# Two sums of the first two experts put off to later experts, the ranking of the experts inside the first gather, and the first four weight reloads singly

## The chip, the cores and the metric

The kernel runs on one core of a Trainium2 chip. Its time is device microseconds (us) of one execution; the times given are medians over runs. An expert's weights come from the chip's memory by DMA into the core's on-chip buffers; the matrix products run on TensorE (PE in the profile, PEld for its weight loads), element work on VectorE (DVE), ScalarE (ACT) and GpSimd (POOL); SyncE (SP) issues the weight DMAs, each when the buffer that it fills is free.

## The reference, cut to what matters

The program is a two-layer block (recurrent mixer, attention, two dense MLPs) followed by a third block (two attention-like branches, an output projection, a layer norm) and a mixture of experts (MoE). Sequence 256, width 1024, 32 experts, 4 experts for each token, all in float32. The change lies in the last part:

```
h = layer_norm(DEEPNORM_ALPHA * h + mix, ln1_g, ln1_b)
logits = h @ router_w + router_b
top_vals, top_idx = lax.top_k(logits, TOP_K)          # 4 of 32
gates = softmax(top_vals)
for each expert e, for the tokens routed to it:
    hcat = x @ w_up[e] + b_up[e]                      # 1024 -> 2048
    x_glu = minimum(hcat[:, 0::2], 7)
    x_lin = clip(hcat[:, 1::2], -7, 7)
    act = x_glu * sigmoid(1.702 * x_glu) * (x_lin + 1)
    y = act @ w_down[e] + b_down[e]                   # 1024 -> 1024
ffn = sum over a token's experts of gate * y
out = layer_norm(DEEPNORM_ALPHA * h + ffn, ln2_g, ln2_b)
```

All 32 experts' weights are read whole: 32 x 12 MB (8 MB up, 4 MB down).

## The kernel before, in words

Up to about 820 us of the span the dense layers run. Their weights are split into high and low parts (L406, L428) and multiplied in three products (L508 to L510); none of that is changed. What follows is the MoE, written for one expert after another in an order fixed at build time; a place in that order is called a position, 0 to 31.

**The work of a position.** U(p) is the first layer of position p: `first_layer` multiplies 64 token slots (`xT`) by eight chunks of the up weights, 1 MB each (L1777 into `hp`), after a product that lays the bias down (`first_bias`, L1577, which needs the one-hot column `sel`). D(p) is the second layer: four chunks of the down weights (L1838 into `py`). `PHASES` orders them U0, U1, D0, U2, D1, U3, D2 and so on. Behind U(p) TensorE turns the gates (`pG`, L1762) and gathers the tokens of position p+1 (`gather`, L1746 into `pX`), which DVE then scales into `xT` (L1749, L1750, in two halves). `gated` is the activation, `turned` its transpose (`paT`, L1820), `keep` scales D(p)'s result into `y` and `combine` adds it to the residual `x` (L1860 into `pC`, then DVE L1861).

**The stream of weights.** Chunks are numbered in the order of use (`ORDER`). The first 20 (20 MB) are loaded by `fill` while the dense layers still run, each as soon as some buffer is free. From then on chunk n goes into the buffer of chunk n-20 (`slots`), and `release(j)`, called behind each chunk's products, issues that load on SP (`load_to`, `load_chunk` L345). Buffers in `paired` take two chunks in one 2 MB DMA, so such a load is issued only when TensorE is through with both chunks of the pair. Chunk 20 is the first of position 2, whose expert number comes out of a table in memory (`ids`), read by SP at L365.

**Hooks.** `later[(p, j)]` lists functions called behind chunk j of position p (j from 8 on is the second layer). They hold the side work: `number_experts` (the table `ids`), `first_gather` (gather of position 0 in three pieces), `three_parts` (`x` split into three bf16 parts for the later gathers), `gates_of_tokens`, `by_token` and `by_position` (the token lists in the order of the positions, `prg` and `prp`), `residual_sum` (`x` times ln1's gain and a constant; the gain is spread over rows by products `pg`, L1924), `start_sum` (the down biases and ln1's bias added to `x` by products `pbd`, L1934, from `rows`, which POOL loads at L1995 and L1996), and `list_overflow`. `rank_experts` (products `pcnt`) orders the experts by token count; it stands between the first gather's second piece and U0.

**The end.** `sums` copies `x` into four PSUM banks by products with the identity (`fin`, L2110), `join` adds D30's result there, `last_norm` adds D31's and computes the last layer norm on DVE. A loop follows for experts with more tokens than slots.

Of the kernel before, what the change touches and what calls it, by code (L numbers as in the profile page):

```python
# [145 lines left out]
def fused(ctx: ExitStack, tc: tile.TileContext, d, out, dbg=None):  # L146
# [173 lines left out]
    stream = {"next": 0}  # L320
    chunk_of, expert_of, paired = {}, {}, []

# [33 lines left out]
    def load_to(n):  # L356

        while stream["next"] < min(n, 12 * NE):
            i = stream["next"]
            pl = slots[i % len(slots)]  # L360
            if pl in paired and n < i + 2:
                break
            pos, j = ORDER[i]
            if j == 0 and pos >= 2:
                e = sp.value_load(ids[0:1, pos:pos + 1], min_val=0, max_val=NE - 1)  # L365
                expert_of[pos] = ds(e, 1)
            stream["next"] += load_chunk(pl, pos, pos if pos < 2 else expert_of[pos], j)
# [850 lines left out]
    with ExitStack() as mixo, ExitStack() as attn:  # L1218
# [232 lines left out]
        paired.append(first)  # L1451
        fill((0, first), (2, first))
        state["ahead"] = 3
# [5 lines left out]
        assert state["loaded"] == TAKEN, (state["loaded"], len(plan))  # L1459
        fill((4, second), (6, parts_A[0]))  # L1460
        act.activation(gates[0], gates[0], AF.Sigmoid)
# [23 lines left out]
        paired.append(third)  # L1485
        fill((10, third))
        mb = ctx.enter_context(tc.tile_pool(name="bias", bufs=1, side="right", reuse_waits="tile"))
# [11 lines left out]
        paired.append(rawD)  # L1499
        fill((8, rawD))  # L1500
        n3 = mo.tile([128, 3, 2, D], BF, name="n3")
# [181 lines left out]

        keep_warm(4)
        pr = mm("prk").rearrange("p (a e) -> p a e", e=NE)
# [11 lines left out]
    slots = [first] * 4 + [second] * 2 + [parts_A[0]] * 2 + [rawD] * 2 + [third] * 2 + [parts_A[1]] * 2 + \  # L1697
        [rawC] * 2 + [parts_A[2], rawF] + [rawE] * 2
    stream["next"] = len(slots)

# [28 lines left out]
    def three_parts(t):  # L1729

        for c in range(2):
            s = slice(c * 512, (c + 1) * 512)
            r = wk.tile([128, 512], F32, name="r", tag=("xl", "sgm")[c], bufs=1)
            hi, mid, lo = [n3[:, i, t, s] for i in range(3)]
            act.copy(hi, x[:, t, s])
            dve.tensor_sub(r, x[:, t, s], hi)
            act.copy(mid, r)
            dve.tensor_sub(lo, r, mid)

# [123 lines left out]
    def rank_experts():  # L1863

        dve.tensor_copy(M4[:, :, 1:4], M[:, :, None, :].to_broadcast([128, 2, 3, NE]))
# [52 lines left out]
    def residual_sum():  # L1918

        for c in range(2):  # L1920
# [5 lines left out]
            for t in range(2):  # L1926
                dve.scalar_tensor_tensor(x[:, t, s], x[:, t, s], ALPHA, gain, op0=OP.mult, op1=OP.mult)

    def start_sum(c):

        s = slice(c * 512, (c + 1) * 512)
        for t in range(2):
            p = mm("pbd")
            pe.matmul(p, RGT[:33, 1, t * 128:(t + 1) * 128], rows[:33, s], start=True, stop=True)  # L1934
            dve.tensor_add(x[:, t, s], x[:, t, s], p)
# [95 lines left out]
    def first_of(n, pos):  # L2031
# [4 lines left out]
        def release(j):  # L2036
# [77 lines left out]
    def last_norm(y, PT, root):  # L2114
# [81 lines left out]
    with tc.For_i(0, n_over, 1) as i:  # L2196
# [53 lines left out]
```

## Time and profile before

| | |
|---|---|
| median of 3 runs | 1771.46 us (1770.03 to 1773.47) |
| the profiled execution | 1773.43 us |
| its span, first to last instruction | 1771.6 us |
| busy: PE / DVE / ACT / POOL | 95% / 52% / 29% / 4% |
| bytes read | 535.37 MB |
| DMA rate in the slices from 930 to 1725 us | 424 to 427 GB/s |

A slice of the page is 1/40 of the span, 44.3 us. The profiled execution lies 2.0 us above the median, inside the spread of the three runs.

### The profile page before, as it was taken

How to read it: one execution, taken by the hardware profiler on the slowest of the kernel's cores; microseconds unless marked ns; L12 is line 12 of the kernel's file. 1: busy time of each engine (PE TensorE's matmuls, PEld its weight loads, DVE VectorE, ACT ScalarE, POOL GpSimd, SP SyncE). 2: the span in 40 equal slices, each digit the busy share in tenths (PEclk: the TensorE clock that was granted, in tenths of full speed). 3: DMA queues.
4: the chain of work that ended last, by engine and by line, in shares of the span. 5: the costliest groups of instructions: out<-in, count | busy, mean ns of one | idle time of the engine just before them, and what ended most of it. 6: DMA issues, size and time to landing. Idle time of an engine off the chain costs nothing.

```text
span 1771.6 us, 27831 instructions
## 1 busy us (share of the span) xinstructions
PE 1678.9 (95%) x11563; PEld 1110.3 (63%) x11563; DVE 929.6 (52%) x1710; ACT 515.1 (29%) x795; POOL 67.2 (4%) x87
## 2 busy tenths in 40 slices
PE   8999999989999999999999999989999998888896
PEld 8899998888999999997433333433333333333332
DVE  7775658678666667775444433324343332323233
ACT  5744444545444455543110011001011010101011
POOL 4020000001000001110000000000000000000000
PEclk9999999999999999999999999999999999999998
DMA  8375554333555544478999999999999999999995
GB/s 276 119 241 184 179 181 149 120 113 130 187 188 185 177 158 151 155 285 322 360 414 425 425 425 427 424 425 427 424 426 425 427 425 426 426 426 426 424 425 222
DMA packets 94370, 538.27 MB, mean 304 GB/s; under 512 B 7088, under 2 KB 20560, under 8 KB 67232
## 3 DMA queue, kind: packets, MB, share of 16 engines
q1 hardware_dynamic: 93360, 534.42, 76.6%
q0 software_dynamic: 736, 1.95, 0.4%
q8 instruction: 93, 1.52, 0.3%
q14 instruction: 37, 0.30, 0.0%
q10 hardware_dynamic: 144, 0.07, 0.0%
HBM read 535.37 MB, written 1.05 MB: 303 GB/s over the span
## 4 chain that ended last, share of the span: by engine, by line
PE 67%; DMA 21%; DVE 7%; ACT 3%; issue 1%; POOL 1%; SPq 0%; ACTq 0%; DVEq 0%; POOLq 0%
PE hp L1777 15%; DMA raw<-in_expert_w_up_dram 10%; PE py L1838 9%; PE pf L508 5%; PE pf L510 5%; PE pf L509 5%; DMA area<-in_expert_w_up_dram 4%; DMA raw<-in_expert_w_down_dram 4%; PE a L508 4%; PE a L510 4%; PE a L509 4%; DMA area<-in_expert_w_down_dram 2%; PE pX L1746 2%; DVE wl L406 1%; PE a L865 1%; PE pC L1860 1%
## 5 line engine op out<-in xcount | busy, mean ns | idle before, releaser
L1777 PE MATMUL hp<-raw,xT 128*64 128x512 f32 x1600 | 365.9, 601 | 20.6 <-DMA raw<-in_expert_w_up_dram 19.8
L406 DVE TENSOR_TENSOR wl<-area,wh 128x1024 fp32r<-128x1024 f32 (+1 forms) x235 | 285.2, 1232 | 142.2 <-ACT wh L428 140.2
L428 ACT CAST wh<-area 128x1024 fp32r<-128x1024 f32 (+1 forms) x238 | 242.2, 1039 | 174.5 <-PE pf L509 95.6
L510 PE MATMUL pf<-hH,wl 128*128 128x256 f32 x928 | 260.8, 281 | 7.7 <-DVE wl L406 7.7
L508 PE MATMUL pf<-hH,wh 128*128 128x256 f32 x928 | 262.9, 283 | 0.1
L509 PE MATMUL pf<-hL,wh 128*128 128x256 f32 x928 | 259.8, 280 | 0.0
L1777 PEld LDWEIGHTS hp<-raw,xT 128*64 128x64 f32 x1600 | 108.9, 137 | 235.1 <-issue 197.5
L1838 PE MATMUL py<-raw,aT 128*64 128x512 f32 x776 | 177.6, 603 | 6.9 <-DMA raw<-in_expert_w_down_dram 6.4
L510 PEld LDWEIGHTS pf<-hH,wl 128*128 128x128 f32 x928 | 175.0, 189 | 9.6 <-DVE wl L406 9.5
L508 PEld LDWEIGHTS pf<-hH,wh 128*128 128x128 f32 x928 | 175.0, 189 | 0.8 <-ACT wh L428 0.5
L509 PEld LDWEIGHTS pf<-hL,wh 128*128 128x128 f32 x928 | 174.8, 188 | 0.1
L1850 ACT ACTIVATE y<-py,gcol 64x512 fp32r<-64x512 f32 x66 | 45.1, 683 | 410.8 <-PE py L1838 367.0
L1851 DVE SCALAR_TENSOR_TENSOR y<-py,gcol,y 64x512 fp32r<-64x512 f32 x66 | 49.6, 751 | 217.6 <-ACT y L1850 217.5
L510 PE MATMUL a<-aH,wl 128*128 128x256 f32 x512 | 145.0, 283 | 0.0
L508 PE MATMUL a<-aH,wh 128*128 128x256 f32 x512 | 144.9, 283 | 0.0
L509 PE MATMUL a<-aL,wh 128*128 128x256 f32 x512 | 144.9, 283 | 0.0
L1861 DVE TENSOR_TENSOR x<-x,pC 128x512 f32<-128x512 f32 x124 | 76.8, 681 | 100.5 <-PE pC L1860 100.5
L1777 PE MATMUL hp<-area,xT 128*64 128x512 f32 x512 | 117.9, 598 | 7.8 <-DMA area<-in_expert_w_up_dram 7.6
L1838 PEld LDWEIGHTS py<-raw,aT 128*64 128x64 f32 x776 | 53.7, 139 | 113.8 <-issue 96.6
L1764 DVE TENSOR_REDUCE gcol<-pG 128x1 f32<-128x256 f32 x33 | 14.0, 424 | 187.6 <-PE pG L1762 187.6
L1822 ACT COPY aT<-paT 128x256 f32<-128x256 f32 x66 | 21.4, 375 | 277.8 <-PE paT L1820 277.8
L508 PEld LDWEIGHTS a<-aH,wh 128*128 128x128 f32 x512 | 98.3, 192 | 0.0
(498 smaller groups left out, 2307.9 us busy)
## 6 DMA issues: line engine op xcount, KB each, us to landing
raw<-in_expert_w_up_dram SPq DMA_DIRECT2D x91, 2048.0 KB, 31.7
raw<-in_expert_w_down_dram SPq DMA_DIRECT2D x43, 2048.0 KB, 33.4
area<-in_mlp_w_dram SPq DMA_DIRECT2D x64, 1024.0 KB, 5.4
area<-in_expert_w_up_dram SPq DMA_DIRECT2D x25, 2048.0 KB, 29.6
area<-in_expert_w_down_dram SPq DMA_DIRECT2D x13, 2048.0 KB, 34.3
area<-in_w_in_dram SPq DMA_DIRECT2D x22, 1024.0 KB, 5.2
area<-in_fox_w_in_dram SPq DMA_DIRECT2D x12, 1024.0 KB, 5.3
area<-in_expert_w_up_dram SPq DMA_DIRECT2D x12, 1024.0 KB, 31.3
```

The source lines that it names most:

```text
L406: e.tensor_sub(wl, src, wh)
L428: act.copy(wh[:, q], src[:, q])
L508: pe.matmul(out_ap, lh, rh, start=first, stop=False, skip_group_check=True)
L509: pe.matmul(out_ap, lh, rl, start=False, stop=False, skip_group_check=True)
L510: pe.matmul(out_ap, ll, rh, start=False, stop=last, skip_group_check=True)
L1746: pe.matmul(p[:, k], n3p[:, i, t, k // 2, k % 2], P[:, t], start=(i + k + t == 0), stop=(i == 2 and t == 1), skip_group_check=True)
L1777: pe.matmul(hp[b][64 * g:64 * g + 64], xT[:, k], w[:, c0:c0 + 512], start=False, stop=(k == KT - 1), skip_group_check=True)
L1822: act.copy(aT[:, i:i + 2], p[:, i:i + 2])
L1838: pe.matmul(py[c], aT[:, j, g * 64:(g + 1) * 64], w[:, i * D + c * 512:i * D + c * 512 + 512], start=(kt == 0), stop=(kt == KT - 1), skip_ ...
L1850: act.activation(y[0:64, s], py[c], AF.Copy, scale=gcol[h])
L1851: dve.scalar_tensor_tensor(y[64:128, s], py[c], gcol[h], y[0:64, s].bitcast(F32), op0=OP.mult, op1=OP.subtract)
L1861: dve.tensor_add(x[:, t, s], x[:, t, s], p)
```

## The change

Seven edits, all in the MoE.

1. `slots` and `fill` are dealt out anew: position 0's first four chunks lie in the two pair buffers of the shared weight area (`parts_A`), and the four loads into them (chunks 20 to 23, `one_by_one`) are 1 MB each, issued behind single chunks instead of pairs.
2. `rank_experts` runs behind the first piece of the first gather, and `number_experts` before U0 instead of behind its chunk 0. The copy of the choice `M` that ranking reads is made earlier, and three more products keep TensorE busy ahead of `prk`.
3. `three_parts` for both halves, with its ACT and DVE steps interleaved, and then `gates_of_tokens` stand behind chunks 0 and 1 of U0 instead of 2, 3 and 4.
4. The column `sel` of position 1 is made behind chunk 5 of U0 instead of after the gather.
5. `residual_sum` moves from position 1 to (2, 1). `start_sum` moves from (1, 7) to (4, 7), and the load of its `rows` by POOL with the gates' transpose (`biases`) to (4, 4).
6. At the end `sums` moves to (31, 5) and (31, 6), two each; one of `turned`'s calls moves one chunk forward.
7. `last_norm` copies its input `fin` back to `x` by ACT (four copies), so that the overflow loop starts from it.

```diff
@@ fills @@
-        fill((0, first), (2, first))
+        fill((4, first), (6, first))
-        fill((4, second), (6, parts_A[0]))
+        fill((0, parts_A[0]), (8, second))
...
-        fill((12, parts_A[1]), (16, parts_A[2]))
+        fill((2, parts_A[1]), (16, parts_A[2]))
@@ load_to @@
-            pl = slots[i % len(slots)]
+            pl = one_by_one.get(i, slots[i % len(slots)])
...
+    slots = [parts_A[0]] * 2 + [parts_A[1]] * 2 + [first] * 4 + [second] * 2 + [rawD] * 2 + [third] * 2 + \
+    one_by_one.update({len(slots) + n: Part(n if n < 2 else n + 1, 1) for n in range(4)})
@@ before U0 @@
-        keep_warm(4)
+        keep_warm(7)
...
-    first_gather(P0, ready[0]["xT"], (slice(0, 2), slice(2, 5)))
-    rows = wk.tile([128, D], F32, name="rows", tag="y", bufs=1)
-    pool.dma_start(rows[:NE], d["expert_b_down_2"][0])
-    pool.dma_start(rows[32:33], d["ln1_b_2"])
-    rank_experts()
+    first_gather(P0, ready[0]["xT"], (slice(0, 2),))
+    rank_experts()
+    first_gather(P0, ready[0]["xT"], (slice(2, 5),))
+    number_experts()
     later = {
-        (0, 0): [number_experts],
-        (0, 1): [lambda: first_gather(P0, ready[0]["xT"], (slice(5, 8),))],
-        (0, 2): [lambda: three_parts(0)],
-        (0, 3): [lambda: three_parts(1)],
-        (0, 4): [gates_of_tokens],
+        (0, 0): [lambda: three_parts(0), lambda: three_parts(1)],
+        (0, 1): [lambda: first_gather(P0, ready[0]["xT"], (slice(5, 8),)), gates_of_tokens],
+        (0, 5): [lambda: sels.append(select(Q[:, :, 1:2]))],
         (1, 1): [by_token],
         (1, 3): [by_position],
-        (1, 4): [residual_sum],
-        (1, 7): [lambda: start_sum(0), lambda: start_sum(1)],
+        (2, 1): [residual_sum],
+        (4, 4): [biases],
+        (4, 7): [lambda: start_sum(0), lambda: start_sum(1)],
@@ new @@
+    def biases():
+        rows = wk.tile([128, D], F32, name="rows", tag="y", bufs=1)
+        pool.dma_start(rows[:NE], d["expert_b_down_2"][0])
+        pool.dma_start(rows[32:33], d["ln1_b_2"])
+        gates = wk.tile([128, 2, S], F32, name="gates", tag="xT")
+        pool.memset(gates[32:33, 1], ALPHA)
+        prg = mm("prg")
+        for t in range(2):
+            pe.transpose(prg[:32, t * 128:(t + 1) * 128], RG[:, 1, t], ident)
+        act.copy(gates[:32, 1], prg[:32, :S])
+        summed.extend([rows, gates])
@@ first_of @@
-            if j == 5 and go_on:
+            if j == (4 if pos == NE - 1 else 5) and go_on:
...
-        select_next(n)
+        if pos:
+            select_next(n)
@@ the end @@
+        for t, c in ((0, 0), (0, 1), (1, 0), (1, 1)) if root else ():
+            act.copy(x[:, t, halves_of[c]], fin[t, c])
-    later[NE - 1, 6] = [lambda: sums([(1, 0), (1, 1)])]
-    later[NE - 2, KT] = [last_gate, lambda: sums([(0, 0)])]
-    later[NE - 2, KT + 1] = [lambda: sums([(0, 1)])]
+    later[NE - 1, 5] = [lambda: sums([(1, 0), (1, 1)])]
+    later[NE - 1, 6] = [lambda: sums([(0, 0), (0, 1)])]
+    later[NE - 2, KT] = [last_gate]
```

On TensorE, from the first gather (`pX`) to the end of U0, before:

```order
L1720 MATMUL pX<-P_8832,x 128x64 x10
L1867 LDWEIGHTS route_b
L1867 MATMUL pcnt<-M_8685,route_b 128x32
L1868 LDWEIGHTS route_b
L1868 MATMUL pcnt<-M_8685,route_b 128x32
L1870 LDWEIGHTS M_8685
L1870 MATMUL pcnt<-route_b,M_8685 128x1
L1870 LDWEIGHTS M_8685
L1870 MATMUL pcnt<-route_b,M_8685 128x1
L1777 MATMUL hp<-raw,xT 64x512 x4
L1887 MATMUL pid<-Q,cf 1x32
L1777 MATMUL hp<-raw,xT 64x512 x4
```

and the same place after the change, up to U0's chunks 0 and 1 (`hp<-area`):

```order
L1722 MATMUL pX<-P_8835,x 128x64 x4
L1869 LDWEIGHTS route_b
L1869 MATMUL pcnt<-M_8685,route_b 128x32
L1870 LDWEIGHTS route_b
L1870 MATMUL pcnt<-M_8685,route_b 128x32
L1872 LDWEIGHTS M_8685
L1872 MATMUL pcnt<-route_b,M_8685 128x1
L1872 LDWEIGHTS M_8685
L1872 MATMUL pcnt<-route_b,M_8685 128x1
L1722 MATMUL pX<-P_8835,x 128x64 x6
L1889 MATMUL pid<-Q,cf 1x32
L1780 MATMUL hp<-area,xT 64x512 x8
```

The ranking products now have six gather products behind them, and `pid` (the expert numbers) stands ahead of U0.

On TensorE, position 1's first layer (from the bias `hp<-bup` to the gates `pG`), before:

```order
L1577 MATMUL hp<-bup,sel 128x512 x2
L1777 MATMUL hp<-raw,xT 64x512 x8
L1894 MATMUL prg<-ident,RG 32x128 x4
L1777 MATMUL hp<-raw,xT 64x512 x8
L1901 MATMUL prp<-Q,RGT 128x32 x4
L1777 MATMUL hp<-area,xT 64x512 x4
L1924 MATMUL pg<-ident,V 128x128 x8
L1777 MATMUL hp<-area,xT 64x512 x4
L1820 MATMUL paT<-ident,xl 128x128 x4
L1777 MATMUL hp<-raw,xT 64x512 x8
L1934 MATMUL pbd<-rows,RGT 128x512 x4
L1762 MATMUL pG<-ident,G 128x128 x2
```

and position 4's first layer after the change, where `pbd` now stands (position 1 keeps the other rows, without `pg` and `pbd`):

```order
L1577 MATMUL hp<-bup,sel 128x512 x2
L1780 MATMUL hp<-raw,xT 64x512 x16
L1863 MATMUL pC<-y,PT 128x512 x4
L1780 MATMUL hp<-raw,xT 64x512 x4
L1940 MATMUL prg<-ident,RG 32x128 x2
L1780 MATMUL hp<-raw,xT 64x512 x4
L1823 MATMUL paT<-ident,xl 128x128 x4
L1780 MATMUL hp<-raw,xT 64x512 x8
L1950 MATMUL pbd<-rows,gates 128x512 x4
L1765 MATMUL pG<-ident,G 128x128 x2
```

The four `pbd` products follow chunk 7 as before, three positions later, with two transposes (`prg`) of their own.

On TensorE, the last position, from U31's chunk 6 to D31's last products, before:

```order
L1777 MATMUL hp<-raw,xT 64x512 x4
L2110 MATMUL fin<-x,ident 128x512 x2
L1777 MATMUL hp<-raw,xT 64x512 x4
L1762 MATMUL pG<-ident,G 128x128 x2
L1838 MATMUL py<-area,aT 64x512 x4
L2110 MATMUL fin<-x,ident 128x512
L1838 MATMUL py<-raw,aT 64x512 x4
L2110 MATMUL fin<-x,ident 128x512
L1838 MATMUL py<-raw,aT 64x512 x4
L1820 MATMUL paT<-ident,xl 128x128 x4
L1838 MATMUL py<-raw,aT 64x512 x12
L2161 MATMUL fin<-y,PT 128x512 x4
```

and after the change, from U31's chunk 5:

```order
L1780 MATMUL hp<-raw,xT 64x512 x4
L2123 MATMUL fin<-x,ident 128x512 x2
L1780 MATMUL hp<-raw,xT 64x512 x4
L2123 MATMUL fin<-x,ident 128x512 x2
L1780 MATMUL hp<-raw,xT 64x512 x4
L1765 MATMUL pG<-ident,G 128x128 x2
L1841 MATMUL py<-area,aT 64x512 x4
L1841 MATMUL py<-raw,aT 64x512 x8
L1823 MATMUL paT<-ident,xl 128x128 x4
L1841 MATMUL py<-raw,aT 64x512 x4
L1841 MATMUL py<-area,aT 64x512 x8
L2177 MATMUL fin<-y,PT 128x512 x4
```

Two of the four `fin` products move ahead of chunk 6, the other two ahead of chunk 7, and none is left between the second layer's chunks.

## Rows read from the trace of the kernel before

**Rows 1.** The page's slices: what the DMA moved, 40 slices of 44.3 us.

```profile
GB/s 276 119 241 184 179 181 149 120 113 130 187 188 185 177 158 151 155 285 322 360 414 425 425 425 427 424 425 427 424 426 425 427 425 426 426 426 426 424 425 222
```

**Rows 2.** Windows: stretch, its length, busy times, TensorE clock, DMA share, GB/s.

```profile
836.00:900.00 64.00, 61.25 (x354) 25.84 (x352) 28.94 (x70) 11.38 (x20) 0.00 (x0) 0.95 0.91 355
876.00:884.00 8.00, 8.00 (x66) 4.33 (x66) 3.37 (x9) 0.00 (x0) 0.00 (x0) 0.59 0.61 260
904.00:1740.00 836.00, 784.48 (x4712) 296.86 (x4710) 311.26 (x739) 86.08 (x182) 0.00 (x0) 0.99 1.01 426
```

**Rows 3.** Timeline of TensorE, positions 0 and 1: start, duration, idle before.

```profile
828.16 0.18 PE L1686 MATMUL prk<-M,route_b 128*128 128x32 bf16 x1 [0.95 <-DVE M L1630]
...
832.62 0.20 PE L1870 MATMUL pcnt<-route_b,M 128*128 128x1 bf16 x2 [0.93 <-DVE M L1865]
...
849.56 0.43 PE L1762 MATMUL pG<-ident,G 128*128 128x128 f32 x2 [0.85 <-DVE G L1755]
849.86 1.56 PE L1746 MATMUL pX<-P,n 128*128 128x64 bf16 x48
853.33 0.73 PE L1577 MATMUL hp<-bup,sel 128*128 128x512 f32 x2 [1.90 <-DVE sel L2016]
853.99 3.65 PE L1777 MATMUL hp<-raw,xT 128*64 128x512 f32 x16
...
864.57 2.05 PE L1924 MATMUL pg<-ident,V 128*128 128x128 f32 x16
...
872.69 4.29 PE L1934 MATMUL pbd<-rows,RGT 33*128 33x512 f32 x8
...
877.38 2.77 PE L1746 MATMUL pX<-P,n 128*128 128x64 bf16 x48
880.08 3.11 PE L1838 MATMUL py<-area,aT 128*64 128x512 f32 x8
...
888.27 0.73 PE L1577 MATMUL hp<-bup,sel 128*128 128x512 f32 x2
```

**Rows 4.** The same view one position later: gather and second layer at full clock.

```profile
905.20 1.56 PE L1746 MATMUL pX<-P,n 128*128 128x64 bf16 x48
906.70 7.09 PE L1838 MATMUL py<-raw,aT 128*64 128x512 f32 x32
```

**Rows 5.** Timeline of DVE: the table of experts, and position 1's tokens, first half.

```profile
834.88 0.18 DVE L1888 CAST ids<-pid 1x32 int32<-1x32 f32 x1 [0.82 <-PE pid L1887]
...
851.92 0.42 DVE L1750 TENSOR_TENSOR xT<-xT,V 128x256 f32<-128x256 f32 x1
```

**Rows 6.** Loads issued at 888.4, 943.0 and 968.4 us: KB, us to landing.

```profile
raw<-in_expert_w_up_dram SPq DMA_DIRECT2D x1, 2048.0 KB, 10.2
raw<-in_expert_w_up_dram SPq DMA_DIRECT2D x1, 2048.0 KB, 9.6
area<-in_expert_w_up_dram SPq DMA_DIRECT2D x1, 2048.0 KB, 13.6
```

**Rows 7.** DMA issues over the span: weights and two small loads, median us to landing.

```profile
raw<-in_expert_w_up_dram SPq DMA_DIRECT2D x91, 2048.0 KB, 31.7
...
ln<-in_ln_dram SPq DMA_DIRECT2D x2, 512.0 KB, 20.4
...
rows<-in_expert_b_down_dram POOLq DMA_DIRECT2D x1, 128.0 KB, 6.9
```

**Rows 8.** Timeline of TensorE at the end.

```profile
1729.91 1.94 PE L1777 MATMUL hp<-raw,xT 128*64 128x512 f32 x8 [0.58 <-DMA raw<-in_expert_w_up_dram]
1731.78 1.98 PE L2110 MATMUL fin<-x,ident 128*128 128x512 f32 x4
...
1737.80 1.12 PE L2110 MATMUL fin<-x,ident 128*128 128x512 f32 x2
...
1740.72 1.13 PE L2110 MATMUL fin<-x,ident 128*128 128x512 f32 x2
```

**Rows 9.** Timeline of ACT at 820 us: one copy of a PSUM bank.

```profile
820.53 0.59 ACT L1596 COPY x<-a 128x512 f32<-128x512 f32 x1
```

More of the change, by code (lines that the diff above doesn't have):

```diff
@@ L320, in fused @@
     stream = {"next": 0}
-    chunk_of, expert_of, paired = {}, {}, []
+    chunk_of, expert_of, paired, one_by_one = {}, {}, [], {}
     def rows_by(ap, e, n):
@@ L1485, in fused @@
         paired.append(third)
-        fill((10, third))
+        fill((12, third))
         mb = ctx.enter_context(tc.tile_pool(name="bias", bufs=1, side="right", reuse_waits="tile"))
@@ L1499, in fused @@
         paired.append(rawD)
-        fill((8, rawD))
+        fill((10, rawD))
         n3 = mo.tile([128, 3, 2, D], BF, name="n3")
@@ L1692, in fused @@
         spread(P0, RG[:, 0, :, 0:1], 0)
+        dve.tensor_copy(M4[:, :, 1:4], M[:, :, None, :].to_broadcast([128, 2, 3, NE]))
         dump("lg", lg)
@@ L1696, in fused @@
     fill((17, rawF))
-    slots = [first] * 4 + [second] * 2 + [parts_A[0]] * 2 + [rawD] * 2 + [third] * 2 + [parts_A[1]] * 2 + \
+    slots = [parts_A[0]] * 2 + [parts_A[1]] * 2 + [first] * 4 + [second] * 2 + [rawD] * 2 + [third] * 2 + \
         [rawC] * 2 + [parts_A[2], rawF] + [rawE] * 2
+    one_by_one.update({len(slots) + n: Part(n if n < 2 else n + 1, 1) for n in range(4)})
     stream["next"] = len(slots)
@@ L1729, in three_parts @@
     def three_parts(t):
[L1731 to L1738, printed above, removed]
+        halves = [slice(0, 512), slice(512, 1024)]
+        rest = [wk.tile([128, 512], F32, name="r", tag=g, bufs=1) for g in ("xl", "sgm")]
+        for s in halves:
+            act.copy(n3[:, 0, t, s], x[:, t, s])
+        for r, s in zip(rest, halves):
+            dve.tensor_sub(r, x[:, t, s], n3[:, 0, t, s])
+            act.copy(n3[:, 1, t, s], r)
+        for r, s in zip(rest, halves):
+            dve.tensor_sub(n3[:, 2, t, s], r, n3[:, 1, t, s])
     def gather(P, xT):
@@ L1863, in rank_experts @@
     def rank_experts():
-        dve.tensor_copy(M4[:, :, 1:4], M[:, :, None, :].to_broadcast([128, 2, 3, NE]))
         pc = mm("pcnt").rearrange("p (a e) -> p a e", e=NE)
@@ L1927, in residual_sum @@
                 dve.scalar_tensor_tensor(x[:, t, s], x[:, t, s], ALPHA, gain, op0=OP.mult, op1=OP.mult)
+    def biases():
[9 more added lines that the diff above has]
+        summed.extend([rows, gates])
     def start_sum(c):
+        rows, gates = summed
         s = slice(c * 512, (c + 1) * 512)
@@ L1933, in start_sum @@
             p = mm("pbd")
-            pe.matmul(p, RGT[:33, 1, t * 128:(t + 1) * 128], rows[:33, s], start=True, stop=True)
+            pe.matmul(p, gates[:33, 1, t * 128:(t + 1) * 128], rows[:33, s], start=True, stop=True)
             dve.tensor_add(x[:, t, s], x[:, t, s], p)
@@ L1986, in turn_gates @@
         ready[no]["g"] = turned_gates(ready[no]["G"], ready[no]["PT"], psum)
-    waiting = []
-    sels = []
+    waiting, sels, summed = [], [], []
     ready[0] = {"P": P0}
     ready[0]["xT"] = wk.tile([128, KT, SLOTS], F32, name="xT")
-    first_gather(P0, ready[0]["xT"], (slice(0, 2), slice(2, 5)))
-    rows = wk.tile([128, D], F32, name="rows", tag="y", bufs=1)
-    pool.dma_start(rows[:NE], d["expert_b_down_2"][0])
-    pool.dma_start(rows[32:33], d["ln1_b_2"])
+    first_gather(P0, ready[0]["xT"], (slice(0, 2),))
+    rank_experts()
+    first_gather(P0, ready[0]["xT"], (slice(2, 5),))
+    number_experts()
     RGT = wk.tile([128, 2, S], F32, name="RGT", tag="xT")
-    pool.memset(RGT[32:33], ALPHA)
-    rank_experts()
     later = {
-        (0, 0): [number_experts],
-        (0, 1): [lambda: first_gather(P0, ready[0]["xT"], (slice(5, 8),))],
-        (0, 2): [lambda: three_parts(0)],
-        (0, 3): [lambda: three_parts(1)],
-        (0, 4): [gates_of_tokens],
+        (0, 0): [lambda: three_parts(0), lambda: three_parts(1)],
+        (0, 1): [lambda: first_gather(P0, ready[0]["xT"], (slice(5, 8),)), gates_of_tokens],
+        (0, 5): [lambda: sels.append(select(Q[:, :, 1:2]))],
         (1, 1): [by_token],
         (1, 3): [by_position],
-        (1, 4): [residual_sum],
-        (1, 7): [lambda: start_sum(0), lambda: start_sum(1)],
+        (2, 1): [residual_sum],
+        (4, 4): [biases],
+        (4, 7): [lambda: start_sum(0), lambda: start_sum(1)],
         (3, 5): [list_overflow],
@@ L2123, in last_norm @@
             for t in range(2):
-                pe.matmul(fin[t, c], PT[:, t * 128:(t + 1) * 128], y[:, halves_of[c]], start=False, stop=True)
+                if root:
+                    pe.matmul(fin[t, c], PT[:, t * 128:(t + 1) * 128], y[:, halves_of[c]], start=False, stop=True)
                 dve.bn_stats(st[:, t, c], fin[t, c])
@@ L2222, in fused @@
         sums([(t, c) for t in range(2) for c in range(2)])
-        last_norm(y, PT, False)
+        last_norm(None, None, False)
 _INS = ['mlp_w1', 'mlp_w2', 'lru_w_in', 'lru_w_r', 'lru_w_i', 'lru_w_out', 'fox_w_in', 'fox_b_f', 'fox_w_out',
```

## The prediction

> **What bounds the kernel now.** I read the page's slices first. From slice 21 on (930 us) the DMA moves 424 to 427 GB/s without a break [rows 1], and the window 904 to 1740 shows a DMA share of 1.01 at 426 GB/s [rows 2]: there the stream of weights is the bound, and TensorE, though busy, waits for it. So the end is set by two things: when the stream comes into full flow, and what is left to do behind its last byte. The second view is the window 836 to 900, between the first reload and full flow: 64.0 us at 355 GB/s [rows 2]. At 426 GB/s those bytes take 64.0 x 355/426 = 53.3 us, so 10.7 us of DMA time are lost there. Why, the timeline of TensorE says: the buffers are full, a reload is issued only when TensorE has used a chunk, and between position 0 and position 2 TensorE does much that frees no buffer [rows 3]. The DMA share falls to 0.61 at 876 to 884, behind `pbd` and the gather, with TensorE's clock at a mean of 0.59, mostly its lower level of 1.2 GHz [rows 2].
>
> **The change, part by part: positions 0 and 1 on TensorE.** I count how much earlier U2 begins (888.27 before [rows 3]).
> - U0. Before, `pcnt` waits 0.93 for the copy of `M`, and behind it comes chunk 0 [rows 3]. Now that copy stands ahead and the gather's second piece fills the time that ranking takes on DVE; `pid` adds a few hundredths. I take 0.9. The table `ids` was written at 834.88, behind chunk 0 [rows 5]; now `pid` stands ahead of chunk 0, and the first reload needs chunk 0 alone: 0.9 and one chunk (1.8) earlier, 2.7 us. The three added warming products cost nothing: they fall into the 0.95 us in which `prk` waits for `M` [rows 3].
> - The wait for `G`, 0.85 [rows 3]: the splitting and the gates now stand behind chunks 0 and 1 instead of 2, 3 and 4, so they begin two to three chunks earlier (1.8 us each, by U1's row [rows 3]), and the rest of U0 covers them. Gone; nothing else is late there.
> - From the gather's end (849.86 + 1.56 = 851.4) to U1's chunk 0 (853.99) is 2.6 us [rows 3], since `sel` is made behind all of `xT` and the bias follows it. Now `sel` is there, the bias falls into the wait, and chunk 0 needs `xT`'s first half, which was ready at 852.34 [rows 5]: 0.9 us behind the gather. 1.65 saved.
> - `pg` (2.05, with 0.05 of overlap 2.0) and `pbd` (4.29, with overlap 4.2) leave position 1 [rows 3].
> - The clock. It fell in `pbd`'s stretch, so the gather took 2.77 and D0 about 8.2 (880.08 to 888.27); at full clock, one position later, they take 1.56 and 7.09 [rows 3, 4]. With `pG` and overlaps, 2.6 saved, if the clock does not fall elsewhere in these two positions; the waits that are left there are under 1 us.
>
> Sum: 0.9 + 0.85 + 1.65 + 2.0 + 4.2 + 2.6 = 12.2 us by U2's start, at about 876.
>
> **What the stream makes of it.** A 2 MB load takes 4.9 us in full flow (2.097 MB at 426 GB/s). The one issued at 943.0 landed 9.6 us later, inside the unbroken stretch; the one issued at 888.4 took 10.2, inside the broken one [rows 2, 6]. So a load that is issued less than about 10 us before its turn to land leaves a gap, and lands about 10 us after its release. Three releases can bind.
> - U1's second chunk frees a pair at 854.2 (853.99 - 3.4, the sum of the first three items, + 3.6); it lands at about 864.4. From there five pairs (chunks 30 to 39) follow 4.9 apart, since their releases come earlier than needed: 889.0. Before, chunk 39 landed at 888.4 + 10.2 = 898.6 [rows 6]. 9.6 us.
> - Position 2 now holds `pg`: from there TensorE is 12.2 - 2.0 = 10.2 us ahead. D2's first pair, released at 943.0 before, is released at 932.8 and lands 9.6 to 10.2 later; before, at 952.6 [rows 6]. 9.6 to 10.2 us. Ahead of it stands `list_overflow` on DVE, which the change leaves alone.
> - Position 4 now holds two transposes (0.3, as long as two of `pG`'s at full clock) and `pbd`: 4.29 as it was, partly at the lower clock, and not under half of that [rows 3]. D3's first pair was released at 968.4 and landed 13.6 later, at 982.0 [rows 6]. Now it is released at 968.4 - 10.2 + 2.4 to 4.6 = 960.6 to 962.8 and lands 9.6 to 10.2 later: 970.2 to 973.0, or 9.0 to 11.8 us earlier. `rows` must be there: U4's last chunk ended 5.4 before that release (a pair, the gather and `pG`: 3.6 + 1.5 + 0.3), at 963.0, and `combine` 7.9 before that (four chunks and a transpose); 10.2 earlier that is POOL's issue at about 945 and the need at about 953. The load took 6.9 before [rows 7], so it is just covered.
>
> The smallest decides. I take the lower end of the third, 9.0 us, because nothing says that `pbd` keeps its full clock there. Behind position 4 TensorE has slack again.
>
> The four single reloads cost two more DMAs. In the stream a 1 MB load adds half of what a 2 MB load adds, by bytes, so I take 0; if each were to cost a start of its own the price is what a 2 MB load pays beyond its flow time when it finds the queue short, 10.2 - 4.9 = 5.3 us [rows 6], once or twice, and all of it before the second and third releases above, which bind anyway. That is the rival "singles" below. The Trainium skill (DMA: Bandwidth & Descriptors, Anatomy of one DMA — SWDGE (gpsimd) path) gives, for loads issued by POOL, a fixed cost of some 2.0 us for each DMA beside its bytes, which speaks against smaller loads. By it, if nothing overlapped, two more would take 4 us (an estimate from that page) and the forecast would lie 4 us later; the unbroken flow of rows 2 shows no such cost when loads are queued.
>
> **The end.** From 1729.91 TensorE does not wait for weights any more, so each product there counts [rows 8]. `fin` takes 1.98 + 1.12 + 1.13 = 4.2 us behind that point. Now two (1.98) stand ahead of chunk 6, where 0.58 was idle, and push it 1.3 later; two (1.95) stand behind it. 4.2 - 1.95 - 1.3 = 0.9 saved. The four ACT copies (4 x 0.59 = 2.4 us [rows 9]) run beside DVE's last norm, in which ACT has one small step; I take 0. If the two engines took turns at these banks it would be 2.4 later.
>
> Sum: 9.0 + 0.9 = 9.9 us. From the profiled execution, 1773.43, that is 1763.5; that execution lies 2.0 above the median, and against the median of 1771.46 it gives 1761.6.
>
> **Rivals.**
> - *The clock falls at `pbd` in position 4.* For it: it fell there before. Against: before, two waits of 0.85 and 1.90 us stood ahead in 25 us [rows 3]. The gather then takes 1.2 us longer, D3's pair up to 1.1, `pG` 0.2, all ahead of the third release: 6.5 us from the stream, 0.9 from the end, 1764.1. Chance 0.3.
> - *Singles.* The first reloads leave gaps of 5.3 us and the later releases do not hide them: 9.7 - 5.3 = 4.4, with the end 5.3 us, 1766.2. Chance 0.07.
> - *The stream does not move,* because buffers are freed no earlier than before at some later place (`list_overflow`'s stretch on DVE, where TensorE waits already). Only the end's 0.9 remains: 1770.6. Against: that stretch begins with a product of TensorE's own order and moves with it. Chance 0.06.
> - *Slower: `rows` comes late.* It is now loaded in full flow. `ln`, behind the weights in SP's queue, took 20.4 us where `rows`, in POOL's, took 6.9 [rows 7]. Each us beyond 8 holds TensorE at `pbd` and D3's release with it; beyond about 18 us the 9.9 are used up. At 20.4 the time is 1774; at the weights' median of 31.7 [rows 7] it is 1771.5 + 13.7 = 1785. Against: POOL's queue is its own, and its 6.9 were taken while weights were being loaded too. Chance 0.05.
>
> **The numbers.** Forecast 0.52, the rivals as given. This kernel's measurement tells 0.2% (3.5 us) from no change: faster is below 1768.0. The forecast, the clock and the singles lie there, with the spread of the runs (1.5 us) taking 0.02: faster 0.87. The stream that stays, those 0.02 and two fifths of the late `rows` are the same: 0.10. Slower: 0.03. The likeliest case alone reaches from 1759.5 (9.6 from the stream, with the lowest run) to 1763.5. The range adds the clock and the singles with 2 us for spread and copies: 1759 to 1767.5.
>
> **What would show it.** Right: the window 836 to 900 at over 400 GB/s; U2's bias near 876; no wait before `pG` and under 0.5 us before U1's chunk 0; `pbd` at about 953 with no idle before it; chunk 39 landed near 889; the last weights some 9 us earlier; no `fin<-x` behind U31. Wrong: a DMA share below 0.95 in 940 to 980 (clock or `rows`), an idle time before `pbd` of several us, or `ln`-like landings of `rows`. If U2 begins at 876 and the end does not move, the rule of the 10 us is wrong.

## The result, and the profile after

The changed kernel took 1762.07 us (median; 1759.85 to 1763.68) beside 1771.57 us for the kernel before (1770.03 to 1773.47): a ratio of 0.9945, 95% interval 0.9928 to 0.9962. A second measurement (below) gave 0.9951 (0.9934 to 0.9968), 1763.57 us. It is faster, by about the 9.9 us of the forecast. The traces put the change itself at 7.4 to 8.0 us; the rest lies within the scatter of the times (see "The sum", below).

The profiled execution took 1763.67 us, its span is 1761.9. The page's slices, 44.0 us each, answer to [rows 1]:

```profile
GB/s 278 120 243 185 178 179 154 120 111 131 190 183 182 182 150 166 135 297 331 412 425 417 426 426 425 424 426 419 418 426 425 426 425 426 426 425 426 424 426 230
```

The slice of 837 to 881 us, number 20, now holds 412. Windows (stretch, length, busy times of PE, PEld, DVE, ACT and POOL, TensorE's clock, DMA share, GB/s), against [rows 2]:

```profile
836.00:900.00 64.00, 63.58 (x428) 26.23 (x426) 23.00 (x64) 6.83 (x15) 0.00 (x0) 1.00 1.00 414
876.00:884.00 8.00, 8.00 (x44) 3.88 (x40) 6.05 (x14) 0.83 (x2) 0.00 (x0) 1.00 1.03 433
904.00:1730.00 826.00, 777.80 (x4622) 294.95 (x4620) 308.97 (x732) 84.72 (x181) 1.35 (x3) 0.99 1.01 424
...
940.00:980.00 40.00, 39.03 (x196) 15.54 (x198) 15.78 (x35) 3.85 (x9) 1.35 (x3) 0.91 1.00 414
...
952.00:960.00 8.00, 8.00 (x61) 4.51 (x61) 4.00 (x9) 0.00 (x0) 0.00 (x0) 0.57 1.01 430
```

The hole behind position 1 is closed: 414 GB/s where 355 stood, the clock full where it had a mean of 0.59. The low clock is now at 952 to 960, at and behind the postponed `pbd`; the DMA share stays at 1.00 in 940 to 980, but the rate is 414 GB/s there. Timeline of TensorE, the rows that answer to [rows 3, 4, 8] (start, duration, idle before and what ended it):

```profile
825.88 0.18 PE L1686 MATMUL prk<-M,route_b 128*128 128x32 bf16 x1
...
845.17 0.44 PE L1765 MATMUL pG<-ident,G 128*128 128x128 f32 x2
...
846.85 0.72 PE L1577 MATMUL hp<-bup,sel 128*128 128x512 f32 x2
847.99 3.65 PE L1780 MATMUL hp<-raw,xT 128*64 128x512 f32 x16 [0.42 <-DVE xT L1753]
...
864.83 1.56 PE L1749 MATMUL pX<-P,n 128*128 128x64 bf16 x48
...
873.34 0.74 PE L1577 MATMUL hp<-bup,sel 128*128 128x512 f32 x2
...
877.59 2.05 PE L1926 MATMUL pg<-ident,V 128*128 128x128 f32 x16
...
922.20 0.69 PE L1765 MATMUL pG<-ident,G 128*128 128x128 f32 x2 [4.35 <-DVE G L1758]
922.68 2.61 PE L1749 MATMUL pX<-P,n 128*128 128x64 bf16 x48
925.22 7.09 PE L1841 MATMUL py<-area,aT 128*64 128x512 f32 x32
...
942.92 0.39 PE L1940 MATMUL prg<-ident,RG 128*32 128x128 f32 x2
...
950.41 5.31 PE L1950 MATMUL pbd<-rows,gates 33*128 33x512 f32 x8 [0.96 <-DMA rows<-in_ln_b_dram]
955.65 0.69 PE L1765 MATMUL pG<-ident,G 128*128 128x128 f32 x2
956.13 2.77 PE L1749 MATMUL pX<-P,n 128*128 128x64 bf16 x48
958.83 7.20 PE L1841 MATMUL py<-raw,aT 128*64 128x512 f32 x32
...
1715.15 1.94 PE L1780 MATMUL hp<-raw,xT 128*64 128x512 f32 x8 [1.25 <-DMA raw<-in_expert_w_up_dram]
...
1738.78 1.20 PE L2177 MATMUL fin<-y,PT 128*128 128x512 f32 x4
```

The same places of the kernel before, as far as they are not in [rows 3, 4, 8]:

```profile
934.99 0.69 PE L1762 MATMUL pG<-ident,G 128*128 128x128 f32 x2 [4.35 <-DVE G L1755]
935.47 2.77 PE L1746 MATMUL pX<-P,n 128*128 128x64 bf16 x48
938.17 8.23 PE L1838 MATMUL py<-raw,aT 128*64 128x512 f32 x32
...
964.75 3.65 PE L1838 MATMUL py<-area,aT 128*64 128x512 f32 x16
...
1725.00 3.65 PE L1777 MATMUL hp<-area,xT 128*64 128x512 f32 x16 [1.27 <-DMA area<-in_expert_w_up_dram]
...
1749.63 0.74 PE L2161 MATMUL fin<-y,PT 128*128 128x512 f32 x2
```

Two traces are best compared from a common instruction on. `prk` started at 828.16 before [rows 3] and at 825.88 after, though nothing ahead of it that matters was changed. I therefore count from `prk`, and cut the rest at two more places: the start of U31's chunks 4 and 5 (the last place where TensorE waits over 1 us for weights; the expectations call it chunk 5), and `join`, the `fin` product with D30's result.

| us | before | after | gain |
|---|---|---|---|
| start of the span to `prk` | 828.16 | 825.88 | 2.28 |
| `prk` to U31's chunks 4 and 5 (the stream) | 896.84 | 889.27 | 7.57 |
| from there to `join` (TensorE's work at the end) | 24.63 | 23.63 | 1.00 |
| `join` to the end of the span | 22.0 | 23.1 | -1.1 |

So the change brought 7.5 us between these two traces; 2.3 us more lay ahead of it.

Loads of the changed kernel, in order: weights issued at 851.68, 873.45 and 962.64 us, then `rows` with ln1's bias by POOL at 941 (KB, us to landing), against [rows 6, 7]:

```profile
raw<-in_expert_w_down_dram SPq DMA_DIRECT2D x1, 2048.0 KB, 11.4
...
raw<-in_expert_w_up_dram SPq DMA_DIRECT2D x1, 2048.0 KB, 14.3
...
raw<-in_expert_w_up_dram SPq DMA_DIRECT2D x1, 2048.0 KB, 9.5
...
rows<-in_expert_b_down_dram POOLq DMA_DIRECT2D x1, 128.0 KB, 7.6
rows<-in_ln_b_dram POOLq DMA_DIRECT2D x1, 4.0 KB, 8.3
```

### The profile page after: what moved, and what is told of

Its sections match the earlier page's. It is cut to its first block, busy times and chain, and to the rows that moved or that the text cites. A ratio compares the mean times of both kernels' runs of the same rounds, so it can differ in the third digit from the quotient of the medians.

```text
span 1761.9 us, 27866 instructions
## 1 busy us (share of the span) xinstructions
PE 1676.2 (95%) x11571; PEld 1109.7 (63%) x11571; DVE 929.2 (53%) x1710; ACT 517.6 (29%) x800; POOL 67.3 (4%) x87
## 4 chain that ended last, share of the span: by engine, by line
PE 72%; DMA 17%; DVE 6%; ACT 2%; issue 1%; POOL 1%; SPq 0%; ACTq 0%; DVEq 0%; POOLq 0%
PE hp L1780 18%; DMA raw<-in_expert_w_up_dram 10%; PE py L1841 9%; PE pf L508 6%; PE pf L510 6%; PE pf L509 6%; DMA raw<-in_expert_w_down_dram 4%; PE a L508 4%; PE a L510 4%; PE a L509 4%; DMA area<-in_expert_w_down_dram 2%; PE pX L1749 2%; DVE wl L406 1%; PE pC L1863 1%; PE a L865 1%
## 5 line engine op out<-in xcount | busy, mean ns | idle before, releaser
L1841 PE MATMUL py<-raw,aT 128*64 128x512 f32 x776 | 173.7, 596 | 5.9 <-DMA raw<-in_expert_w_down_dram 4.9
```

The source lines that it names most:

```text
L1841: pe.matmul(py[c], aT[:, j, g * 64:(g + 1) * 64], w[:, i * D + c * 512:i * D + c * 512 + 512], start=(kt == 0), stop=(kt == KT - 1), skip_ ...
```

## The experiments

All are the changed kernel with the edit shown, unless another is named. Times scatter by some 3 us about a median, so where less matters I read the trace, in the three distances of the table above.

| kernel | median us | ratio to before, 95% | `prk` at | to U31 4/5 | to `join` | to the end |
|---|---|---|---|---|---|---|
| before, second trace | 1771.06 (one run) | | 825.8 | 896.83 | 24.62 | 22.0 |
| again | 1763.57 | 0.9951 (0.9934 to 0.9968) | 825.6 | 889.06 | 23.63 | 22.8 |
| sums_back | 1767.45 | 0.9974 (0.9963 to 0.9986) | 827.1 | 891.34 | 23.63 | 22.9 |
| defer_only | 1770.45 | 0.9980 (0.9968 to 0.9991) | 826.0 | 892.66 | 24.63 | 22.0 |
| pbd_twice | 1771.38 | 0.9987 (0.9975 to 0.9998) | 824.7 | 898.55 | 23.62 | 22.9 |
| sums_later | 1764.94 | 0.9953 (0.9938 to 0.9968) | 829.2 | 888.42 | 23.63 | 22.7 |
| pairs | 1763.04 | 0.9947 (0.9931 to 0.9964) | 826.2 | 889.16 | 23.63 | 21.7 |
| later_pairs | 1762.78 | 0.9938 (0.9923 to 0.9953) | 828.5 | 889.14 | 23.63 | 21.8 |
| no_copies | 1765.83 | 0.9956 (0.9939 to 0.9973) | 826.9 | 889.12 | 23.62 | 22.7 |
| pad1 | 1765.66 (one run) | | 828.5 | 888.84 | 23.63 | 22.9 |
| pad2 | 1762.86 (one run) | | 825.4 | 889.13 | 23.63 | 23.0 |

The kernel before had medians of 1771.91 us beside again, sums_back, pairs and no_copies, and of 1772.85 us beside the other four with a ratio. Beside the three single runs it took 1768.99 us, once.

### Are the traces' distances the program's own?

Two unaltered kernels. The changed one:

> The changed kernel once more, unaltered, so that the three beside it have a reference of the same chip. If the gain is the change's own: 1760 to 1764 us, a ratio of 0.993 to 0.996, with U2's bias 47.5 us behind `prk` and the last weights about 111.7 + 802 us behind it, as in the first run. If a good part of the gain were a quieter early part of the program (the dense part was 2.3 us shorter in the profiled run): 1764 to 1767.

and the kernel before:

> The kernel before once more, for a second trace of it. If the times behind `prk` are the program's own: last weights 921.5 +- 0.4 us behind `prk`, last `fin` 7.8 behind them, last output 10.9 behind that, execution over 3.2 us later; `prk` itself anywhere from 824.7 to 829.2, as in nine traces of kernels that share the part ahead of it. If the traces of before and after differ by chance in the stream: over 1 us off 921.5.

They are. Before repeats 896.83, 24.62 and 22.0; after repeats 889.06, 23.63 and 22.8. Only `prk` moves: 824.7 to 829.2 over all traces, with no order between kernels. In the two traces of before it stands at 828.2 and 825.8. The second execution of before (span 1769.3) and the changed kernel (1761.9), `prk` within 0.1 us in both, differ by 7.4 us. The medians of the two measurements differ by 9.5 and 8.3, with intervals that reach down to 6.7 and 5.7 (0.0038 and 0.0032 of the time before): the traces' 7.4 lies in both. The repeated run met its expectation: 1763.57 us, and U2's bias 47.5 us behind `prk`.

### The postponed sums back in position 1

```diff
-        (2, 1): [residual_sum],
-        (4, 4): [biases],
-        (4, 7): [lambda: start_sum(0), lambda: start_sum(1)],
+        (1, 4): [residual_sum],
+        (1, 7): [lambda: start_sum(0), lambda: start_sum(1)],
```

(with the load of `rows` and `RGT` as before)

> The changed kernel with the row products and the bias sums back in position 1 and `rows` loaded early again. Theory (what counts is TensorE's lead in positions 0 and 1): `pg`, `pbd` and the clock's fall return, 2.0 + 4.2 + up to 2.6 us of the 12.2, U2 begins 6 to 9 us later than in the changed kernel, the stream loses 4 to 7 of its 7.6, and the time is 1766 to 1769. Rival (the postponed work costs in position 4 what it saved in position 1, the gain is the early ranking and the singles): within 1.5 us of the changed kernel.

Rows of its trace, two of TensorE and two windows:

```profile
827.08 0.18 PE L1686 MATMUL prk<-M,route_b 128*128 128x32 bf16 x1 [0.29 <-DVE M L1630]
...
881.78 0.74 PE L1577 MATMUL hp<-bup,sel 128*128 128x512 f32 x2
```

```profile
836.00:900.00 64.00, 63.57 (x408) 27.11 (x408) 25.18 (x66) 8.03 (x16) 0.00 (x0) 0.97 0.97 388
876.00:884.00 8.00, 8.00 (x38) 2.61 (x36) 1.36 (x4) 1.28 (x2) 0.00 (x0) 1.00 0.83 285
```

U2 begins 54.7 us behind `prk`, 7.2 later than with the sums postponed, the hole is half back (388 GB/s, DMA share 0.83 at 876 to 884), and the stream is 2.1 us later: less than the 4 to 7 expected. The time, 1767.45, lies in the range given, but 3.9 above again where the trace says 2.1. The rival is out: U2 and the hole followed the sums.

### The postponed sums alone

The kernel before with that part of the diff only.

> The kernel before with the postponed sums alone (`pg` at position 2, `rows`, `pbd` at position 4); ranking, splitting, `sel`, reloads and the end as before. Undoing this part in the changed kernel put the start of U31's chunk 5 2.1 us later (behind `prk`) of 7.6 gained. Theory (the early parts bring the stream to the same unbroken flow, so their gains don't add): U2 8 to 9 us earlier, chunk 39 of the weights some 6 us earlier, the stream 4.5 to 6 us earlier, and with nothing won at the end 1766 to 1768 us. Rival (the gains add): the stream gains 7.6 - 5.5 = 2.1, 1769.5 to 1770.5.

The stream gains 4.2 us (896.84 to 892.66), U2 8.9 (60.1 to 51.2 behind `prk`). The other edits alone gained 5.5 (896.84 to 891.34, in sums_back). Together 9.7, where both at once give 7.6: they overlap, by 2.1 us, less than the theory had it and not nothing, as the rival had it. The end stays at 24.63: its 1.00 us comes with the other edits, of which `sums` is the one at this place. The time doesn't follow the trace here: the median, 1770.45, is 2.4 us below its kernel before (interval 1.6 to 5.7), outside the theory's 1766 to 1768 and inside the rival's range. The trace's 4.2 lies within the interval, so the overlap of 2.1 us is read from traces alone, and the times don't confirm it.

### Each bias product twice

```diff
-            pe.matmul(p, gates[:33, 1, ...], rows[:33, s], start=True, stop=True)
+            for _ in range(2):
+                pe.matmul(p, gates[:33, 1, ...], rows[:33, s], start=True, stop=True)
```

> The changed kernel with each of the four bias products `pbd` given twice (the first of each is overwritten), which adds 3.5 us to position 4 at full clock and 5.3 at the lower one. Theory (the third release has under 1 us of slack): D3's loads are released 3.5 to 5.3 us later, a gap of 2.5 to 4.5 us opens in the stream, and the last weights land as much later: 1766 to 1768. Rival (the stream's lead hides position 4, so postponing cost nothing there and there is room for more): under 0.5 us.

Its row of TensorE, and the window behind it:

```profile
950.34 13.13 PE L1951 MATMUL pbd<-rows,gates 33*128 33x512 f32 x16 [2.00 <-DMA rows<-in_ln_b_dram]
```

```profile
940.00:980.00 40.00, 38.00 (x163) 14.93 (x164) 11.31 (x27) 3.21 (x7) 1.35 (x3) 0.79 0.79 318
```

`pbd` grew by 7.8 us instead of 3.5 to 5.3, the wait for `rows` by 1.0: 8.9 us. The stream ends 9.3 us later (898.55). All of it came through, and the time, 1771.38, missed the theory's 1766 to 1768 for it. So position 4 has no room left: what is added there is paid in full. That says nothing yet of what already stands there.

### Bias sums at position 8

```diff
-        (4, 4): [biases],
-        (4, 7): [lambda: start_sum(0), lambda: start_sum(1)],
+        (8, 4): [biases],
+        (8, 7): [lambda: start_sum(0), lambda: start_sum(1)],
```

> The changed kernel with `rows` and `pbd` at position 8 in place of 4. Theory (the third release was at its limit: in the repeated run a load of D3's stretch landed exactly 10.0 us after its issue and 0.65 us behind its turn): the last weights 0.5 to 1.2 us earlier behind `prk` than 913.75 to 914.0, window 940 to 980 at full clock, time 1 us less at most. Rival A (the flow's start sets all): 913.8 +- 0.3. Rival B (`pbd` and the low clock had no slack at all in position 4): 2.5 us or more earlier.

The window that the expectation names:

```profile
940.00:980.00 40.00, 40.00 (x255) 15.61 (x252) 16.59 (x41) 4.34 (x10) 0.00 (x0) 1.00 1.00 424
```

The clock is full and the stream is 0.6 to 0.85 us earlier (888.42 against 889.06 and 889.27), as the theory said. The time is not shorter (1764.94). D3 begins here 125.8 us behind `prk`, 7.1 earlier than in the changed kernel:

```profile
955.06 7.09 PE L1841 MATMUL py<-raw,aT 128*64 128x512 f32 x32
```

So of what stands in position 4 hardly any reached the stream: something else holds it 0.6 to 0.85 us further on. The stream isn't without breaks behind position 4 either. Three fences show it: sums_later at the new place of `rows` (POOL issues it at 1047.6 us) and again some 375 to 425 us behind `prk`; then that later place in the changed kernel; then the same in the kernel before:

```profile
1050.00:1055.00 5.00, 5.00 (x27) 1.79 (x24) 0.00 (x0) 0.65 (x2) 0.00 (x0) 1.00 1.00 361
1205.00:1255.00 50.00, 47.26 (x270) 17.79 (x267) 15.20 (x36) 4.76 (x10) 0.00 (x0) 0.97 1.00 419
```

```profile
1200.00:1250.00 50.00, 47.25 (x248) 17.36 (x246) 16.82 (x40) 5.16 (x11) 0.00 (x0) 0.97 0.99 412
```

```profile
1200.00:1250.00 50.00, 45.80 (x284) 18.11 (x286) 21.06 (x53) 5.58 (x12) 0.00 (x0) 0.97 1.01 427
```

The first dip went with `rows` from position 4 to this place: at a full DMA share 5 x (426 - 361)/426 = 0.8 us of the DMA's time are lost, beside the 0.3 us of the 132 KB themselves. The second came with the postponed sums: sums_back, without them, has 424 GB/s at 1200 to 1250.

### Single reloads or pairs

```diff
-    one_by_one.update({len(slots) + n: Part(n if n < 2 else n + 1, 1) for n in range(4)})
```

> The changed kernel with the first four reloads as two pairs of 2 MB. Theory (the singles neither cost nor gain: two chunks of 1 MB are there about when one load of 2 MB would be): within 1.0 us of the changed kernel. Rival A (the gaps of 5.3 and 2.9 us before the second reload's landing are the singles' cost, and were the stream's missing 1.4 us): 1.5 to 3 us faster. Rival B (the earlier first reload is part of the gain): 1.5 to 2 us slower, since the first reload is issued one chunk, 1.8 us, later.

889.16 against 889.06 and 889.27: the singles neither cost nor give anything in the stream. In the Trainium skill's model for loads issued by POOL (DMA: Bandwidth & Descriptors, Anatomy of one DMA — SWDGE (gpsimd) path) two more DMAs would cost 4 us (the estimate in the prediction); no run here shows any of it for queued 1 MB loads on SyncE's queue. The run settles another question by chance:

```profile
951.63 3.67 PE L1949 MATMUL pbd<-rows,gates 33*128 33x512 f32 x8 [0.62 <-DMA rows<-in_ln_b_dram]
...
955.71 2.77 PE L1748 MATMUL pX<-P,n 128*128 128x64 bf16 x48
```

Here `pbd` ran at full clock, 1.6 us shorter, and D3 began 0.8 us earlier behind `prk` (958.41 - 826.22 = 132.2, against 958.83 - 825.88 = 133.0), yet the stream ended where it did. pad1 and pad2 (below), which have the pairs too, agree: `pbd` 3.73 and 3.67, the stream 888.84 and 889.13. So the fall of the clock at `pbd` costs the stream nothing that can be told from its scatter.

Both edits at once:

> The sums at position 8 and the first four reloads as two pairs. Theory (neither binds by more than 1 us): within 1.2 us of the changed kernel, 1761.5 to 1764, the last weights 912.6 to 914.0 us behind `prk`. Rival (both are worth something and add): 2 us or more faster.

889.14, though D3 began as early as in sums_later: the 0.6 to 0.85 us did not come again, so they are within what the flow scatters. Its median, 1762.78, is the lowest of all but not to be told from 1763.57 and 1763.04.

### The copies, and what did grow at the end

```diff
-        for t, c in ((0, 0), (0, 1), (1, 0), (1, 1)) if root else ():
-            act.copy(x[:, t, halves_of[c]], fin[t, c])
```

> The changed kernel without ACT's four copies behind the last norm (the branch for overflows adds its product again, as in the kernel before). Theory (the copies cost at the end: from the last output's landing to the end of the execution it took 4.4 us in the changed kernel and 3.2 before): 0.8 to 1.5 us faster. Rival (they run beside the last norm and cost nothing; the longer end is scatter): within 0.4 us.

The theory falls: without the copies the end is as long (22.7 us behind `join`, 22.8 and 23.1 with them), the time not shorter (1765.83, within the scatter of 1763.57). But it was 21.7 in pairs, which has the copies. The trace's semaphore records on SyncE show the difference behind the last output: in every kernel with the singles its last row of semaphore instructions stands still, between the ninth and the tenth, for 1.4 to 1.7 us; without the singles it runs through. Two kernels tell whether the loads or the length of SyncE's program does it; they are pairs with one and with two more readings of the expert's number:

```diff
                 expert_of[pos] = ds(e, 1)
+                for _ in range(1 if pos == 3 else 0):
+                    sp.value_load(ids[0:1, pos:pos + 1], min_val=0, max_val=NE - 1)
```

> The changed kernel with its first four reloads as two pairs, and one more reading of the expert's number on SyncE at position 3 (three instructions; SyncE's program has then 724 in place of 721, with the singles 725). In all six traces of kernels with the singles, SyncE's last row of semaphore instructions stood still for 1.4 to 1.7 us in the middle, behind its ninth, and the last output was followed by 4.0 to 4.35 us; without the singles 2.9 to 3.2, without that stop. Theory (the stop hangs on where in SyncE's program the row lies, so longer programs bring it nearer): the stop returns, behind the tenth, and 4.0 to 4.4 us follow the last output. Rival (it belongs to the two more loads and their semaphores): no stop, 2.9 to 3.2 us.

> As the run before, with two more readings (727 instructions). Theory: the stop stands behind the seventh semaphore instruction, 4.0 to 4.4 us follow the last output. Rival (the two more loads): no stop, 2.9 to 3.2 us.

With either the end is long again (22.9 and 23.0 us behind `join`; 4.1 and 4.2 behind the last output), though the loads are pairs. The stop was not where I had counted it: behind the row, 1.4 us at a drain, in pad1, and behind the eleventh, 1.5 us, in pad2. What the stop waits for is not shown. The view of DMA queues has one candidate, the loads of instructions. Over 5.5 us, from 0.4 us ahead of the last output's last bytes on, in pairs and then in pad2:

```profile
GB/s 417 343 45 60 0 0 0 0 0 0 0 0 0 0 0 0 60 0 0 0 0 0 0 0 0 0 0 0 0 0 0 0 0 60 0 0 0 0 0 0
...
q14 instruction: 3, 0.02, 1.7%
```

```profile
GB/s 402 343 60 60 0 0 0 0 0 0 0 0 0 0 0 60 0 0 0 0 0 0 0 0 0 0 0 0 0 0 0 0 60 0 0 0 0 0 0 0
...
q14 instruction: 3, 0.02, 1.7%
```

Both have three loads at about the same times, whether SyncE stops or not (in pairs the third falls behind the end of the span). So the stop doesn't come of one more load. In time it fits the second: in the eight traces with a stop the stop begins within 0.3 us of that load's start and ends 1.0 to 1.2 us behind its end. The Trainium skill (Runtime: NRT & Kernel Launch, Instruction fetch mechanics) says that a sequencer's next block comes by DMA and that crossing a boundary is mostly hidden. If the stop is such a crossing, it was not hidden here: it took 1.4 to 1.7 us, and 1.1 us of it shows in the end. That it is one is argued, from the times and from the two kernels with longer programs, and not shown.

## Why the prediction was right or wrong, point by point

- **U2 at about 876, 12.2 us earlier.** Right: 47.46 us behind `prk` against 60.11, 12.65. The signs named for it are there: no wait before `pG` and 0.42 us before U1's chunk 0, the gather at 1.56 and the clock full in this stretch. `ids` is written 4.3 us behind `prk` where it was 6.7 [rows 5], by the timeline of DVE:

```profile
830.21 0.17 DVE L1890 CAST ids<-pid 1x32 int32<-1x32 f32 x1
```

- **The first two releases, 9.6 and 9.6 to 10.2.** About right. Chunk 39 landed at 873.45 + 14.3 = 887.7, 61.9 us behind `prk` against 70.4: 8.6 earlier. The load issued at 851.68 took 11.4 us, not 10.2, since others still lay ahead of it in the queue. At `pG` of position 3 TensorE was 10.5 us ahead (922.20 - 825.88 against 934.99 - 828.16), as forecast (10.2).
- **The third release, 9.0 to 11.8, taken at 9.0.** This is the term that was mis-sized. It charged position 4 with 2.4 to 4.6 us. From that `pG` to D3's first product it took 958.83 - 922.20 = 36.6 us, against 964.75 - 934.99 = 29.8 before: 6.9 us. The rows give it: transposes 0.4, the wait for `rows` 0.96 (forecast: just covered), `pbd` 5.31 (4.29 was taken), gather and `pG` at the low clock 1.2 and 0.25 more, less 1.3 for the gather behind U3 and for D2, where the low clock was shorter (922.68 and 925.22 against 935.47 and 938.17). So D3's load was released 3.5 us earlier behind `prk`, not 5.6; with 9.5 instead of 13.6 us to land, it landed 7.6 us earlier.
- **But it was not what decided.** With position 4 empty D3 began 7 us earlier, and the stream gained 8.4 (sums_later) and 7.7 (later_pairs) in place of 7.6 and 7.8. So what TensorE does in position 4 took at most 0.85 us of the 1.4 that the stream missed, perhaps nothing (the load of `rows` took its dip along to position 8); pbd_twice shows only that it had no room for more. The forecast took its size from a release that hardly binds, and came near in part by luck.
- **What stands behind it.** The forecast looked for the release that binds, and took TensorE to have slack again behind position 4. Two losses had no term: `rows` loaded in full flow takes some 0.8 us of the DMA's time beside its bytes, and some 375 to 425 us behind `prk` the rate falls to 412 GB/s over 50 us where it was 427, 50 x 15/427 = 1.8 us. There TensorE takes a position with two groups of tokens (128 passes of `hp` where the others have 64) and so frees its buffers later. That this is the reason, and how much of either loss reaches the last weights, no run shows.
- **TensorE waits for the stream.** This holds later than the prediction reads it. In the kernel before the view of waits shows no wait of TensorE for weights from 965 to 1400 us; all lie behind that, the largest group:

```profile
PE hp L1777 <- DMA raw<-in_expert_w_up_dram: 19.8, 22, 2.0
```

- **The clock's fall at `pbd`, the rival with 0.3.** The fall came: with the singles `pbd` took 5.31 to 5.53 us (after, again, no_copies), with pairs 3.67 to 3.73 (pairs, pad1, pad2), and the gather behind it 2.77 in after and pairs. The 7.6 us that the stream gained lie between this rival's 6.5 and the forecast's 9.0. But where `pbd` kept the full clock the stream gained no more, so the fall at `pbd` doesn't explain the loss.
- **The singles, nothing taken.** Right for the stream. (The rival's sum starts from 9.7, where the first release gave 9.6.) What they cost, 1.1 us at the end, comes without the loads too, with three or six more instructions on SyncE; no step had it.
- **The end, 0.9.** Right: 1.00 up to `join`. **The copies, nothing taken.** Right, by no_copies. Each waits for DVE's step that reads `fin` (L2146), but runs beside the rest of the last norm and doesn't lengthen it; the first two in ACT's timeline, each 0.58, as in [rows 9]:

```profile
1749.74 0.58 ACT L2171 COPY x<-fin 128x512 f32<-128x512 f32 x1 [0.69 <-DVE area L2146]
1751.85 0.58 ACT L2171 COPY x<-fin 128x512 f32<-128x512 f32 x1 [1.52 <-DVE area L2146]
```

- **`rows` in full flow, the slower rival.** 7.6 and 8.3 us, far from the 20.4 that it would have needed.
- **The sum.** Forecast 9.0 + 0.9 = 9.9. Shown: 7.6 + 1.0 - 1.1 = 7.5. The forecast of 1761.6 lies 0.5 us from the median of the first measurement, and that is partly luck: in it the medians differ by 2.0 us more than the traces. Over the nine measurements with a ratio, the difference of the medians less that of the traces (from `prk` on, against the mean of the two traces of before) runs from -1.9 (no_copies) to 3.1 (pbd_twice), on the mean 0.1. That speaks for scatter, and against a gain ahead of `prk`.

## What to carry to other kernels

Work that is moved out of a hole in the stream is free where it lands only as far as that place has lead to spare. Here 6.9 us stood in the new place and at most 0.85 reached the stream, but the next 8.9 came through whole. So price the new place with the wait for its data and the lower clock behind it, compare that with the lead there, and look for the later places where the stream can break once it runs earlier. Two cures for one hole need not add. Count from a common instruction when two traces are compared: here three distances repeated to 0.3 us, while the whole time scattered by several.

## What the runs showed of the hardware that I had not expected

- A few instructions more on SyncE, far from the end, lengthened the end by 1.1 us, by a stop of 1.4 to 1.7 us on SyncE: 22.7 to 23.1 us behind `join` in eight traces, 21.7 to 22.0 in five.
- A small load can take more from a full stream than its bytes: with `rows` (132 KB) the rate fell to 361 GB/s for 5 us at a DMA share of 1.00 (sums_later): 0.8 us lost, beside the 0.3 us that its bytes take at 426 GB/s.
- Four fp32 products of 33 rows more cost TensorE 7.8 us at this place (5.31 to 13.13), over twice the 3.67 that four take at full clock. All eight at the lower clock would take 4 x 3.67 = 14.7 us (an estimate), so a clock that fell earlier in this run, behind a wait of 2.00 us, is enough to explain it.
- The moment of the clock's fall shifts with little: in pairs the wait ahead of `pbd` was 0.62 us and `pbd` took 3.67, in the changed kernel 0.96 and 5.31. The wait alone doesn't decide: in defer_only it was 0.95, and `pbd` took 3.67.
